# A fused decoder block: four buffers for split weights, later modulation loads on POOL, and accumulator banks that end one by one

## The chip, the cores and the metric

The kernel runs on one core of a Trainium2 chip, as one launch. The metric is the device time of that launch in microseconds (us). The core has several engines that run their own instruction streams: TensorE (PE, matrix products), VectorE (DVE), ScalarE (ACT), GpSimd (POOL) and SyncE (SP). DMA transfers are issued by one of these streams (here SP and POOL) and run beside them. An instruction waits on semaphores until what it needs is there; behind a waiting instruction its whole engine stands.

## The reference

One decoder block over 2048 tokens of width 1024. A vector c sets six modulation vectors (48 columns of 128 values); the first two shift and scale the first normalised input, the others serve the later parts. One combined projection feeds two groups of heads, gated linear attention (GLA) and dilated attention. Their outputs are joined, projected, and a gated feed-forward part follows.

```python
cond = jax.nn.silu(c)
mod = (cond @ w_ada[l] + b_ada[l])[:, None, :]
sh1, sc1, g1, sh2, sc2, g2 = jnp.split(mod, N_MOD, axis=-1)

h = rms_norm(x, norm1_g[l]) * (1 + sc1) + sh1
proj = h @ w_in[l]
gq, gk, gv, gr, glr, aq, ak, av = jnp.split(proj, split_at, axis=-1)
log_a = jax.nn.log_sigmoid((glr @ gla_w_gate[l] + gla_b_gate[l])) / GLA_GATE_TAU
y_gla = gla_group(gq, gk, gv, log_a, gr, gla_norm_g[l])
y_att = dilated_attention_group(qa, ka, av)      # qa, ka: rms_norm of aq, ak
mixed = jnp.concatenate([y_gla, y_att], axis=-1)
x = x + g1 * (mixed @ w_out[l])

h = rms_norm(x, norm2_g[l]) * (1 + sc2) + sh2
u = causal_depthwise_conv(h @ w_up[l], conv_w[l], conv_b[l])
u_gate, u_val = jnp.split(u, 2, axis=-1)
x = x + g2 * ((silu(u_gate) * u_val) @ w_down[l])
```

Widths in the combined projection: gq and gk 256 each, gv and gr 512 each, glr 16, aq, ak and av 512 each; the feed-forward part is 2816 wide.

## The kernel before

*Tiling.* The 2048 tokens are worked in four chunks of 512 (numbered 0 to 3). Activations lie with their 1024 channels as eight tiles of 128 partitions by 512 tokens. A large product is made of three matmuls for each tile (`mm3`, L288 to L290): activation and weight are each split into a high half of reduced precision and the low rest, and high by high, high by low and low by high are summed in one accumulator. The names `hhi`, `hlo` are the halves of an activation, `whi`, `wlo` those of a weight.

*Split weights.* Every weight block comes through `wslot`: a load of 512 KB into one of two raw buffers (`wraw`, L220, issued by POOL), a cast to the high half on ACT (L226), a subtraction for the low half on DVE (L227). The halves stand in three buffers each. `plan` lists all blocks in the order of use; `weights` gives out the next block, and before that starts the preparation of blocks up to `ahead=2` further on in the list. A raw buffer is free again when cast and subtraction have read it; a split buffer is free when the block's last matmuls have read it.

*The projections of one chunk.* `proj` runs the combined projection in an order written out by hand (`ORDER0` for chunk 0, `ORDER` for the others). `q0` to `q7` are queries and keys of the dilated heads (`qk`), `g0` to `g3` queries and keys of GLA (`glaqk`), `V0` and `V1` the values with the gate input (`av`), `W0` is gv and `W1` is gr (`wide`). `ORDER` begins with `W0` and both lists end with `W1`; so W1 of one chunk and W0 of the next one meet. I call this place the hand-over. There are four PSUM banks named `psg` for the accumulators of all large products, taken in turn, and four named `psa` for the small ones. A query or key block takes one `psg` bank; its drain is a square and a copy on ACT.

*wide.* It takes all four `psg` banks, one for each 128 tokens. For each of four weight blocks j, two tiles i, and four banks s, it issues one `mm3`; so each block is 24 matmuls of 128x512. The banks are drained at the end: for W0 by a copy on ACT (L497); for W1 by a tanh on ACT (L493), an addition and multiplication on DVE that reads the bank a last time (L494), and a multiplication by the norm's gain (L495). The result goes to memory by a DMA on SP (L498).

*The next chunk's input.* Between W1's last matmul and its drains, `hook` calls `begin(c + 1)`, which writes the normalisation and modulation of the next chunk: for each of eight tiles a product on DVE (L413), the high half on ACT (L415) and the low half on DVE (L417).

*Later modulation.* Modulation columns 16 to 47 aren't needed by the first projections. `ada_late` computes them beside the projections: 32 columns in two halves each, 64 loads of 128x512 (`wada`, L348, issued by SP) into buffers of the pool that the query blocks and Newton's steps use too (tags `ghi` and `glo`, five buffers each). Each half is multiplied by `cond` and summed on DVE (L355) two steps after its load; after a column's second half its bias is added (L332).

*What sets the order.* The code of the streams is interleaved by generators: `along` and `beside` advance one generator a set number of steps for each step of another. While the projections of chunks 1 to 3 are written, the attention of chunk 0 (`mix`, lines 579 to 800 in what follows) is interleaved with them. A scheduler then fixes the order of instructions on every engine when the program is built (`schedule_with_timeline_sim=True`): it works with modelled durations. So a change of buffers or dependencies moves many instructions on all engines.

After the projections follow, chunk by chunk, the output projection and the feed-forward part, with the attention of the next chunk beside them.

## Time and profile before

| what | value |
|---|---|
| median of three runs | 2660.18 us (2659.1 to 2661.48) |
| the profiled execution, its own time | 2663.11 us |
| its span in the trace | 2661.4 us |
| mean granted clock of TensorE | 0.992 |
| large matmuls in the three forms of `mm3` at 128x512 | 2040 each |
| weight blocks split on ACT and DVE (L226, L227) | 391 |
| moved by software queues (POOL's loads) | 203.71 MB |
| moved by hardware queues (SP's) | 198.40 MB |

The span is what the profiler recorded from the first to the last instruction; the execution's own time is 1.7 us longer. A busy share is an average over a start-up, a stage of projections (about 60 to 740 us), and a long stage of output and feed-forward products. The granted clock is the share of its full rate that TensorE was allowed to run at; the mean hides short stretches at half of it. In the views, `out<-in` are the names of buffers, "x" counts instructions, and "<-" with an engine and a line names what ended a wait.

### The profile page before, as it was taken

Reading aid. Unit: us, or ns where it says so; the run is one execution under the profiler, and the core shown is the slowest. Engines: PE = TensorE matmul, PEld = TensorE weight load, DVE = VectorE, ACT = ScalarE, POOL = GpSimd, SP = SyncE. Lnnn points to the kernel's source line nnn. Section 1 sums busy time; section 2 is a strip of 40 time slices with the busy share of each in tenths; the row PEclk is TensorE's granted clock in tenths of the full one; section 3 lists DMA queues with packets and bytes.
Section 4 is the critical chain, followed back from the end, with each engine's and each line's share of the span. In section 5 each row is a group of like instructions: output and inputs, shape, how many; then the busy total and the mean of one; then the engine's idle time right before and its main releaser. Section 6 shows DMA issues by size and latency. Waiting matters only on the chain.

```text
span 2661.4 us, 46859 instructions
## 1 busy us (share of the span) xinstructions
PE 2583.6 (97%) x18152; PEld 2116.1 (80%) x18152; DVE 1920.8 (72%) x4120; ACT 1274.0 (48%) x2607; POOL 209.1 (8%) x396
## 2 busy tenths in 40 slices
PE   5989999999989999999999999999999999999999
PEld 3877878878868888887787888878888888788887
DVE  7585885766677777776896777779777766666666
ACT  4455556556545454553545444445455443433332
POOL 0000000000000000001000000000000000010000
PEclk9999999999989999999999999999999999999999
DMA  7765575755633234346434444553344445422222
GB/s 281 247 203 200 185 235 168 226 183 191 219 108 103 97 124 132 125 132 227 137 104 125 140 133 129 192 167 118 101 139 145 141 125 186 135 96 102 95 95 95
DMA packets 196736, 405.10 MB, mean 152 GB/s; under 512 B 19985, under 2 KB 70946, under 8 KB 195234
## 3 DMA queue, kind: packets, MB, share of 16 engines
q0 software_dynamic: 55872, 203.71, 23.2%
q1 hardware_dynamic: 140642, 198.40, 22.7%
q8 instruction: 143, 2.34, 0.4%
q14 instruction: 79, 0.65, 0.1%
HBM read 339.12 MB, written 62.91 MB: 151 GB/s over the span
## 4 chain that ended last, share of the span: by engine, by line
PE 82%; issue 5%; DMA 5%; DVE 5%; ACT 2%; POOL 0%; SPq 0%; DVEq 0%; POOLq 0%; ACTq 0%
PE psg L288 24%; PE psg L289 23%; PE psg L290 23%; PE psa L752 2%; PE psa L732 2%; PE psa L854 2%; DMA wada<-in_w_ada_dram 1%; PE psa L590 1%; DVE wlo L227 1%; DMA sq<-in_xT_dram 1%; PE psa L849 1%; DMA x<-x 1%; PE psa L768 1%; DVE x L966 0%; DMA wraw<-in_w_ch_dram 0%
## 5 line engine op out<-in xcount | busy, mean ns | idle before, releaser
L288 PE MATMUL psg<-hhi,whi 128*128 128x512 f32 x2040 | 809.5, 399 | 15.9 <-ACT hhi L415 9.9
L289 PE MATMUL psg<-hlo,whi 128*128 128x512 f32 x2040 | 805.7, 395 | 2.7 <-DVE hlo L417 2.6
L290 PE MATMUL psg<-hhi,wlo 128*128 128x512 f32 x2040 | 804.0, 394 | 0.7 <-DVE wlo L227 0.7
L226 ACT CAST whi<-wraw 128x1024 fp32r<-128x1024 f32 (+1 forms) x391 | 409.9, 1049 | 472.2 <-PE psg L289 396.0
L227 DVE TENSOR_TENSOR wlo<-wraw,whi 128x1024 fp32r<-128x1024 f32 (+1 forms) x391 | 478.6, 1224 | 206.2 <-ACT whi L226 200.6
L288 PEld LDWEIGHTS psg<-hhi,whi 128*128 128x128 f32 x2040 | 385.6, 189 | 105.8 <-ACT hhi L415 13.3
L289 PEld LDWEIGHTS psg<-hlo,whi 128*128 128x128 f32 x2040 | 386.6, 190 | 85.9 <-DVE hlo L417 5.9
L290 PEld LDWEIGHTS psg<-hhi,wlo 128*128 128x128 f32 x2040 | 386.5, 189 | 83.0 <-DVE wlo L227 1.9
L288 PE MATMUL psg<-ghi,whi 128*128 128x512 f32 x704 | 279.5, 398 | 0.0
L289 PE MATMUL psg<-glo,whi 128*128 128x512 f32 x704 | 277.3, 394 | 0.0
L290 PE MATMUL psg<-ghi,wlo 128*128 128x512 f32 x704 | 276.0, 392 | 0.0
L966 DVE SCALAR_TENSOR_TENSOR x<-psg,mod,x 128x512 f32<-128x512 f32 x192 | 142.9, 748 | 117.3 <-PE psg L290 115.4
L288 PE MATMUL psg<-whi,hhi 128*128 128x512 f32 (+2 forms) x512 | 172.8, 347 | 12.3 <-DVE stg L494 7.9
L289 PE MATMUL psg<-wlo,hhi 128*128 128x512 f32 (+2 forms) x512 | 176.2, 345 | 5.7 <-DVE wlo L227 5.7
L220 POOL DMA_DIRECT2D wraw<-in_w_up_dram x176 | 92.9, 528 | 1080.6 <-DVE wlo L227 969.2
L290 PE MATMUL psg<-whi,hlo 128*128 128x512 f32 (+2 forms) x512 | 175.3, 343 | 0.0
L288 PEld LDWEIGHTS psg<-ghi,whi 128*128 128x128 f32 x704 | 132.3, 188 | 32.0 <-issue 4.6
L290 PEld LDWEIGHTS psg<-ghi,wlo 128*128 128x128 f32 x704 | 132.3, 188 | 28.2 <-issue 1.2
L289 PEld LDWEIGHTS psg<-glo,whi 128*128 128x128 f32 x704 | 132.4, 188 | 27.9 <-issue 2.1
L742 ACT ACTIVATE big<-big,nm 128x256 f32<-128x256 f32 (+1 forms) x256 | 122.4, 480 | 58.7 <-DVE nm L757 58.7
L921 ACT ACTIVATE y<-psg,conv_b_sb,conv_w_sb 128x512 f32<-128x512 f32 x176 | 135.8, 773 | 4.8 <-PE psg L290 2.3
L923 DVE SCALAR_TENSOR_TENSOR y<-psg,conv_w_sb,y 128x510 f32<-128x510 f32 x176 | 130.9, 744 | 0.7
(206 smaller groups left out, 3369.5 us busy)
## 6 DMA issues: line engine op xcount, KB each, us to landing
wraw<-in_w_up_dram POOLq DMA_DIRECT2D x176, 512.0 KB, 3.6
wraw<-in_w_down_dram POOLq DMA_DIRECT2D x88, 512.0 KB, 3.5
wraw<-in_w_ch_dram POOLq DMA_DIRECT2D x44, 512.0 KB, 4.5
wada<-in_w_ada_dram SPq DMA_DIRECT2D x74, 256.0 KB, 4.8
v<-v SPq DMA_DIRECT2D x68, 256.0 KB, 5.3
wraw<-in_w_tokw_dram POOLq DMA_DIRECT2D x32, 512.0 KB, 4.4
wraw<-in_w_out_dram POOLq DMA_DIRECT2D x32, 512.0 KB, 4.7
sq<-in_xT_dram SPq DMA_DIRECT2D x48, 256.0 KB, 4.4
```

The lines of the kernel that those rows point to most:

```text
L220: (nc.gpsimd if self.planned else nc.sync).dma_start(raw[:, :n], src)
L226: nc.scalar.copy(hi[:, :n], raw[:, :n])
L227: nc.vector.tensor_tensor(lo[:, :n], raw[:, :n], hi[:, :n].bitcast(F32), op=ALU.subtract)
L288: nc.tensor.matmul(ps, wh, hh, start=first and k == 0, stop=False, skip_group_check=shared)
L289: nc.tensor.matmul(ps, wh, hl, start=False, stop=False, skip_group_check=shared)
L290: nc.tensor.matmul(ps, wl, hh, start=False, stop=k == n - 1, skip_group_check=shared)
L732: nc.tensor.matmul(at(i, hh, z), q[H[hh], i * P:(i + 1) * P], key(H[hh], i, z), start=True, stop=True, skip_group_check=True)
L742: nc.scalar.activation(t[:, lo:hi], t[:, lo:hi], AF.Exp, bias=nm[:, hh, g, i:i + 1], scale=2.0 ** -(h + 1), accum_out=dn[:, hh, g, i:i + 1])
L752: nc.tensor.transpose(ps[:n, i * P:(i + 1) * P], part(S[hh], i), self.C("id"))
L921: nc.scalar.activation(y, ps, AF.Identity, bias=self.cb[:, b:b + 1], scale=self.cw[:, 2, b:b + 1])
L923: nc.vector.scalar_tensor_tensor(y[:, 2:], ps[:, :T - 2], self.cw[:, 0, b:b + 1], y[:, 2:], op0=ALU.mult, op1=ALU.add)
L966: nc.vector.scalar_tensor_tensor(x1, ps, self.mod[:, 40 + cb:41 + cb], x1, op0=ALU.mult, op1=ALU.add)
```

## The change

The diff does five things.

- The split weights have four buffers for each half, and `weights` prepares three blocks ahead (two for the second block of `av`, one before).
- The 64 late modulation loads are issued by POOL, on the queue that loads the weights.
- Each late modulation reduction waits for the matmul that `mm3` issued last when the code of the reduction was written (`self.lastmm`). So a reduction can't be placed ahead of the block beside which it was written.
- In `wide` the last block's eight `mm3` are sorted by bank: both tiles of bank 0, then those of bank 1, 2 and 3. The normalisation of the next chunk (`hook`) is written behind the drains.
- A scratch area for DMA descriptors is set to 4096 bytes, which frees room for the buffers.

```diff
@@ -135,8 +135,8 @@
         pool = lambda name, bufs, **kw: ctx.enter_context(tc.tile_pool(name=name, bufs=bufs, **kw))
         self.const = pool("const", 1)
         self.wraw = pool("wraw", 2)
-        self.whi = pool("whi", 3)
-        self.wlo = pool("wlo", 3)
+        self.whi = pool("whi", 4)
+        self.wlo = pool("wlo", 4)
         self.hp = pool("hp", 9)
         self.gp = pool("gp", 5)
         self.xp = pool("xp", 8)
@@ -268,7 +268,7 @@
                 yield from down(5)
             yield from ffn(c)
 
-    def weights(self, name, *idx, ahead=2):
+    def weights(self, name, *idx, ahead=3):
 
         while len(self.wready) <= self.wpos + ahead and self.wleft:
             n, i, k, m = self.wleft.pop(0)
@@ -287,7 +287,7 @@
             (wh, wl), (hh, hl) = ws[k], hs[k]
             nc.tensor.matmul(ps, wh, hh, start=first and k == 0, stop=False, skip_group_check=shared)
             nc.tensor.matmul(ps, wh, hl, start=False, stop=False, skip_group_check=shared)
-            nc.tensor.matmul(ps, wl, hh, start=False, stop=k == n - 1, skip_group_check=shared)
+            self.lastmm = nc.tensor.matmul(ps, wl, hh, start=False, stop=k == n - 1, skip_group_check=shared)
 
 
     def ada_setup(self):
@@ -345,14 +345,16 @@
             if n < len(parts):
                 b, j = parts[n]
                 raw = self.gp.tile([P, T], F32, name="wada", tag=("ghi", "glo")[j])
-                ld = nc.sync.dma_start(raw, self.A["w_ada"][b][:, cols(j)])
+                ld = nc.gpsimd.dma_start(raw, self.A["w_ada"][b][:, cols(j)])
                 if not n:
                     self.after(ld)
                 raws.append(raw)
             if n >= 2:
                 b, j = parts[n - 2]
                 raw, m = raws[n - 2], self.mod[:, b:b + 1]
-                nc.vector.tensor_tensor_reduce(raw, raw, self.cond[:, cols(j)], 0.5, m if j else 0.0, ALU.mult, ALU.add, m)
+                t = nc.vector.tensor_tensor_reduce(raw, raw, self.cond[:, cols(j)], 0.5, m if j else 0.0, ALU.mult, ALU.add, m)
+
+                self.tc.add_manual_dep(t.ins, self.lastmm.ins.name, mybir.DependencyInfo(mybir.DependencyClass.Sync, mybir.DependencyReason.DATA))
                 if j:
                     self.ada_end(b)
             yield
@@ -478,15 +480,16 @@
             pss = [self.pg() for _ in range(4)]
             for j in range(4):
                 w = self.weights("w_tokw", b, j)
-                for i in range(2):
-                    for s in range(4):
-                        h, l = hs[2 * j + i]
-                        tk = slice(s * P, (s + 1) * P)
-                        self.mm3(pss[s], [(h[:, tk], l[:, tk])], w[i:i + 1], i == 0 and j == 0, True)
+                order = [(i, s) for i in range(2) for s in range(4)]
+                if j == 3:
+
+                    order.sort(key=lambda x: x[1])
+                for i, s in order:
+                    h, l = hs[2 * j + i]
+                    tk = slice(s * P, (s + 1) * P)
+                    self.mm3(pss[s], [(h[:, tk], l[:, tk])], w[i:i + 1], i == 0 and j == 0, True)
                 if j < 3:
                     yield
-            if b == 1 and hook:
-                hook()
             for s in range(4):
                 st = stage()
                 if b:
@@ -496,11 +499,13 @@
                 else:
                     nc.scalar.copy(st, pss[s])
                 nc.sync.dma_start(D["rg" if b else "gv"][s * P:(s + 1) * P, :], st)
+            if b == 1 and hook:
+                hook()
             yield
 
         def av(b):
             n = 256 if b else 272
-            w = self.weights(f"w_av{b}", 0) + self.weights(f"w_av{b}", 1, ahead=1)
+            w = self.weights(f"w_av{b}", 0) + self.weights(f"w_av{b}", 1, ahead=2)
             if b:
                 pss = [self.pg() for _ in range(2)]
                 for i in range(KD):
@@ -1098,7 +1103,7 @@
     from concourse.bass_utils import run_bass_kernel_spmd as _run
 
     arrs = layout(**{n: np.asarray(a) for n, a in inputs.items()})
-    nc = _bacc.Bacc("TRN2", target_bir_lowering=False, num_devices=1)
+    nc = _bacc.Bacc("TRN2", target_bir_lowering=False, num_devices=1, dynamic_dma_scratch_size=4096)
     A = {n: nc.dram_tensor(f"in_{n}_dram", a.shape, mybir.dt.from_np(a.dtype), kind="ExternalInput").ap() for n, a in arrs.items()}
     A["outT"] = nc.dram_tensor("out_0_dram", (NCH, KD, P, T), F32, kind="ExternalOutput").ap()
     with tile.TileContext(nc, **TC) as tc:
```

From L288 on lines are shifted: L413, L415 and L417 of before are L415, L417 and L419 now, L494 is L497 and the copy L497 is L500.

The order of instructions, first on VectorE at the hand-over from chunk 0 to chunk 1, just ahead of the first drain of gr. `wada` is a modulation load's buffer, `mod` the modulation, `sq` and `stg` are staging tiles, `kt` and `sbd` belong to the attention of chunk 0. Before:

```order
L355 ISA wada,mod<-wada,cond 128x512
L355 ISA mod 128x1
L355 ISA wada,mod<-wada,cond,mod 128x512
L355 ISA mod 128x1
L641 COPY sbd_485<-kt 32x2x2x32
L641 COPY sbd_487<-kt 32x2x2x32
L355 ISA wada,mod<-wada,cond,mod 128x512
L355 ISA mod 128x1
L413 SCALAR_TENSOR_TENSOR sq<-sq,G_110,rstd 128x512
L227 TENSOR_TENSOR wlo<-wraw,whi 128x1024
L494 SCALAR_TENSOR_TENSOR stg<-stg,psg 128x512
```

In the changed program, at the same place:

```order
L227 TENSOR_TENSOR wlo<-wraw,whi 128x1024
L332 TENSOR_TENSOR mod<-mod,b_ada_sb 128x1
L355 ISA wada,mod<-wada,cond 128x512
L355 ISA mod 128x1
L579 COPY kt<-psa 128x512
L415 SCALAR_TENSOR_TENSOR sq<-sq,G_110,rstd 128x512
L606 TENSOR_TENSOR kt<-psa,consts_sb 128x128
L455 SCALAR_TENSOR_TENSOR stg<-stg,kgs,sq 128x512
L606 TENSOR_TENSOR kt<-psa,consts_sb 128x128
L497 SCALAR_TENSOR_TENSOR stg<-stg,psg 128x512 x4
```

The low half of a weight stands earlier, one modulation reduction instead of three stands in the rows ahead of the first drain, some of the attention's work has moved there, and the four drains (now L497) stand one behind the other.

Second, POOL's queue from W1 of chunk 0 on. Here `in_w_tokw` are the blocks of W0 and W1, `in_w_av` those of V0 and V1, `in_w_ch` those of queries and keys. Before:

```order
L220 DMA wraw<-in_w_av_dram 128x1024 x2
L220 DMA wraw<-in_w_ch_dram 128x1024 x4
L220 DMA wraw<-in_w_tokw_dram 128x1024 x8
L541 MEMSET glr 32x512
L220 DMA wraw<-in_w_av_dram 128x1088 x2
```

In the changed program (one block of W1 and a modulation load stand ahead of these rows; with it they hold the eight blocks of W1 and W0):

```order
L220 DMA wraw<-in_w_tokw_dram 128x1024 x4
L348 DMA wada<-in_w_ada_dram 128x512
L220 DMA wraw<-in_w_tokw_dram 128x1024
L348 DMA wada<-in_w_ada_dram 128x512 x8
L220 DMA wraw<-in_w_tokw_dram 128x1024
L348 DMA wada<-in_w_ada_dram 128x512
L220 DMA wraw<-in_w_tokw_dram 128x1024
```

Weight loads and modulation loads are mixed now, with up to eight modulation loads ahead of one weight block.

Third, VectorE near the end of W1 of chunk 2, in a stretch beside the attention of chunk 0 (`xm` and `nm` belong to it). Before:

```order
L417 SCALAR_TENSOR_TENSOR hlo<-sq,mod,hhi 128x512
L355 ISA wada,mod<-wada,cond 128x512
L355 ISA mod 128x1
L355 ISA wada,mod<-wada,cond,mod 128x512
L355 ISA mod 128x1
L227 TENSOR_TENSOR wlo<-wraw,whi 128x1024
L332 TENSOR_TENSOR mod<-mod,b_ada_sb 128x1
L417 SCALAR_TENSOR_TENSOR hlo<-sq,mod,hhi 128x512
L227 TENSOR_TENSOR wlo<-wraw,whi 128x1024
```

In the changed program:

```order
L355 ISA wada,mod<-wada,cond 128x512
L355 ISA mod 128x1
L415 SCALAR_TENSOR_TENSOR sq<-sq,G_110,rstd 128x512 x2
L227 TENSOR_TENSOR wlo<-wraw,whi 128x1024
L415 SCALAR_TENSOR_TENSOR sq<-sq,G_110,rstd 128x512
L799 TENSOR_TENSOR xm<-md,consts_sb 128x64
L419 SCALAR_TENSOR_TENSOR hlo<-sq,mod,hhi 128x512 x2
L227 TENSOR_TENSOR wlo<-wraw,whi 128x1024
L497 SCALAR_TENSOR_TENSOR stg<-stg,psg 128x512
```

One reduction instead of two stands ahead of the low halves here, and between the two low halves stand parts of the next chunk's normalisation.

## The prediction

> **What bounds the kernel now.** I read the page's first lines, the waits of TensorE (PE), the windows of the projection stage, and the timelines of PE and VectorE (DVE) there.
>
> ```profile
> span 2661.4 us, 46859 instructions
> PE 2583.6 (97%) x18152; PEld 2116.1 (80%) x18152; DVE 1920.8 (72%) x4120; ACT 1274.0 (48%) x2607; POOL 209.1 (8%) x396
> ```
>
> PE sets the end: it is busy for 97% of the span, so 2661.4 - 2583.6 = 77.8 us is all that it idles. Only that, and stretches at a lower clock, can be won.
>
> ```profile
> PE psa L400 <- DVE rstd L394: 17.5, 2, 14.6
> PE psg L288 <- ACT hhi L415: 9.9, 5, 4.3
> PE psg L288 <- DVE stg L494: 7.9, 3, 5.7
> PE psg L289 <- DVE wlo L227: 5.7, 3, 3.1
> PE psg L288 <- ACT stg L497: 1.9, 2, 1.4
> ```
>
> Each row gives the total, the number and the longest wait. The first two are the start and the change-over to the output projection, which the change does not touch. The other three are its targets: the drain of gr's banks (L494), the low half of a split weight (L227), the drain of gv's banks (L497): 7.9 + 5.7 + 1.9 = 15.5 us.
>
> ```profile
> 60.00:180.00 120.00, 117.45 (x664) 99.53 (x664) 74.70 (x119) 65.66 (x102) 10.04 (x19) 1.00 0.70 230
> 180.00:200.00 20.00, 12.63 (x130) 9.60 (x129) 19.96 (x43) 10.56 (x20) 2.12 (x4) 0.74 0.51 179
> 534.00:550.00 16.00, 11.43 (x46) 8.89 (x47) 12.84 (x25) 12.05 (x28) 1.58 (x3) 0.89 0.46 147
> 2300.00:2600.00 300.00, 299.46 (x1320) 247.38 (x1319) 195.38 (x307) 110.55 (x136) 28.52 (x55) 1.00 0.29 98
> ```
>
> Columns: stretch, length, busy time of PE, weight loads, DVE, ScalarE (ACT) and POOL, PE's granted clock, DMA share, GB/s. From 2300 to 2600 PE idles 0.5 us, so deeper buffering has nothing to win in the last stage. In 180 to 200 DVE is busy 19.96 of 20 us while PE works 12.63: there DVE is the bound. That is the hand-over from W1 of chunk 0 (the gr projection) to W0 of chunk 1 (gv); 534 to 550 is that from chunk 2 to 3.
>
> ```profile
> 182.73 0.76 PE L289 MATMUL psg<-wlo,hhi 128*128 128x512 f32 x1 [1.67 <-DVE wlo L227]
> 195.57 0.79 PE L288 MATMUL psg<-whi,hhi 128*128 128x512 f32 x1 [5.70 <-DVE stg L494]
> 221.02 0.39 PE L288 MATMUL psg<-whi,hhi 128*128 128x272 f32 x1 [1.39 <-ACT stg L497]
> 364.91 0.50 PE L288 MATMUL psg<-whi,hhi 128*128 128x512 f32 x1 [0.49 <-DVE stg L494]
> 535.66 0.50 PE L289 MATMUL psg<-wlo,hhi 128*128 128x512 f32 x1 [3.11 <-DVE wlo L227]
> 544.71 0.80 PE L288 MATMUL psg<-whi,hhi 128*128 128x512 f32 x1 [1.68 <-DVE stg L494]
> ```
>
> In brackets stands PE's wait and what ended it. They come in pairs, a late weight and then a late drain, at 182/195, at 365 and at 535/545. The third weight wait, by the total above, is 5.7 - 1.67 - 3.11 = 0.9 us.
>
> ```profile
> 182.80:186.20 3.40, 3.40 (x8) 2.71 (x9) 3.40 (x9) 0.00 (x0) 0.53 (x1) 0.50 0.70 222
> 193.10:199.80 6.70, 4.23 (x10) 3.36 (x11) 6.70 (x14) 3.39 (x5) 1.06 (x2) 0.50 0.52 196
> 544.70:548.00 3.30, 3.29 (x8) 2.62 (x9) 3.30 (x7) 3.30 (x7) 0.53 (x1) 0.50 0.04 13
> ```
>
> The granted clock is 0.50 in these stretches, which follow the waits of 1.67, 5.70 and 1.68 us. Each of about 3.4 us costs 1.7 us more, the double one up to 3.4.
>
> The Trainium skill ("TensorE: Matmul & The Clock Gate", What's actually happening) lets the clock fall only after a whole idle window of some 3.4 us. By that, the waits of 1.67 and 1.68 us would cost themselves alone, and the 3.4 us of clock in the sum below would be 0 (9.0 us instead of 12.4). The trace shows 0.50 behind both, so the measurement decides.
>
> **The change part by part.** Durations by the distance from one start to the next:
>
> ```profile
> 186.68 0.69 DVE L613 TENSOR_TENSOR pt<-kt,pt 128x512 f32<-128x512 f32 x1
> 187.28 0.69 DVE L614 TENSOR_TENSOR pt<-kt,pt 128x512 f32<-128x512 f32 x1
> 182.60 0.28 DVE L601 TENSOR_TENSOR kt<-psa,consts_sb 128x128 f32<-128x128 f32 x1
> 182.80 0.68 DVE L355 CUSTOM_DVE_ANT_0 wada<-wada,cond 128x512 f32<-128x512 f32 x1
> 533.09 0.69 DVE L355 CUSTOM_DVE_ANT_0 wada<-wada,cond 128x512 f32<-128x512 f32 x1
> 533.70 0.75 DVE L355 CUSTOM_DVE_ANT_0 wada<-wada,cond,mod 128x512 f32<-128x512 f32 x1
> 534.38 1.23 DVE L227 TENSOR_TENSOR wlo<-wraw,whi 128x1024 fp32r<-128x1024 f32 x1
> 535.51 0.16 DVE L332 TENSOR_TENSOR mod<-mod,b_ada_sb 128x1 f32<-128x1 f32 x1
> 535.58 0.75 DVE L417 SCALAR_TENSOR_TENSOR hlo<-sq,mod,hhi 128x512 fp32r<-128x512 f32 x1
> 536.24 1.23 DVE L227 TENSOR_TENSOR wlo<-wraw,whi 128x1024 fp32r<-128x1024 f32 x1
> 194.85 0.67 DVE L494 SCALAR_TENSOR_TENSOR stg<-stg,psg 128x512 f32<-128x512 f32 x1
> 195.45 0.73 DVE L417 SCALAR_TENSOR_TENSOR hlo<-sq,mod,hhi 128x512 fp32r<-128x512 f32 x1
> 362.89 0.39 PE L288 MATMUL psg<-whi,hhi 128*128 128x512 f32 x1
> 363.12 0.39 PE L289 MATMUL psg<-wlo,hhi 128*128 128x512 f32 x1
> 189.11 0.76 PE L590 MATMUL psa<-pt 64*32 64x32 f32 x64
> ```
>
> So a DVE operation on 128x512 takes 0.60 (two full tensors, or a drain L494) or 0.66 (one with a scalar column, L413/L417/L453), a modulation reduction 0.61 or 0.68, a low half 1.13, L601 0.20, a bias 0.07. PE takes 0.23 per 128x512 matmul and 0.76 for 64 small ones.
>
> *Hand-over of chunk 0.* In the changed program the last W1 bank still runs all its 24 matmuls at the end of W1, since it waits for a query bank's copy. The first tied modulation reduction waits for this bank's sixth matmul, 18 before the end. Everything behind it on DVE stands in order: from it to the first drain (L497 now) are three reductions (0.61 + 0.68 + 0.61), two low halves (2.26), five operations of 0.66 (3.30), two of Newton's (1.20), one bias (0.07), a copy from PSUM (0.60), two L606 (0.40) and the drain (0.60): 10.3 us. PE has 18 x 0.23 = 4.1 and 0.6 us of small matmuls meanwhile, so the first matmul of W0 still waits about 10.3 - 4.7 = 5.6, with hand-offs **5.9 us**. Before, it was 1.67 + 5.70 = 7.4: 1.5 us are won. The four drains stand together now and the modulation reductions between them are gone, but the tie itself makes DVE start this run late. The weight wait of 1.67 goes, as the last W1 block's low half now stands ahead of the reductions: 1.7 us of clock are won, the double stretch stays.
>
> *Drain of gv.* The last block's matmuls go bank by bank, so the first bank is done 3 x 6 matmuls = 4.1 us ahead of the last, and its copy on ACT is hidden by them. Both waits go: **1.9 us**.
>
> *Hand-over of chunk 1.* From the end of a run of small matmuls to the first drain stand 17 DVE operations: three low halves (3.39), seven of 0.66 (4.62), three of 0.60, one reduction (0.61), three of 0.20 (0.60): with the drain among the 0.60 about 11.0 us, against 41 matmuls of W1 (9.3) and 1.1 us of small ones: about 0.6 us left of 0.9 + 0.49: **0.8 us**.
>
> *Hand-over of chunk 2.* The low half that PE waited for (534.38) stood behind two reductions; it now stands a block earlier, and from the reduction tied to W1's last block to the drain are 7.0 us of DVE work (0.61, five of 0.66, two of 1.13, 0.22, 0.60) against 42 matmuls and small ones, 10.4 us. Both waits go, 3.11 + 1.68 = **4.8 us**, and 1.7 us of clock.
>
> Sum: 1.5 + 1.7 + 1.9 + 0.8 + 4.8 + 1.7 = 12.4 us won.
>
> *What it adds.* No arithmetic. The 64 late modulation loads move from SP to POOL:
>
> ```profile
> L348 SPq DMA_DIRECT2D wada<-in_w_ada_dram x60: 327/432/1681, 93.7 to 665.2; - x60
> DMA to landing us min/median/max: 2.9/4.5/8.1
> L220 POOL DMA_DIRECT2D wraw<-in_w_tokw_dram x32 | 16.9, 528 | 232.0 <-DVE wlo L227 174.3 <-DVE kt L601 20.0 <-DVE mod L332 19.0
> wraw<-in_w_tokw_dram POOLq DMA_DIRECT2D x32, 512.0 KB, 4.4
> ACT whi L226 <- PE psg L289: 396.0, 183, 9.8
> ```
>
> POOL issues one in 0.53 us: 64 x 0.53 = 34 us on an engine that is busy 8%, hidden by its long waits for a free raw buffer; SP is relieved of 64 x 0.43 = 28 us. Queued behind them are weight loads. The tightest is the third block of W0 behind eight modulation loads: its raw buffer is free 4.3 us after the tied matmul (0.61 + 0.60 + 0.66 + 0.68 + 1.13 and hand-offs), it lands 4.4 later and is cast 1.05 later, at 9.8 us; its first use is 12 matmuls into W0, at 4.7 + 5.9 + 2.7 = 13.3. Cover: 3.5 us; cost taken 0. Without that cover it is the slower rival. The ties add 64 semaphore waits on DVE; no row prices them, the bounds are 0 (DVE has slack outside the hand-overs) and the whole 5.9 us that one costs above; beyond what is counted I take 1.0. Eight reductions more fall in the last chunk's projections, 8 x 0.65 = 5.2 us of DVE beside PE: 0. The smaller descriptor scratch has no row: 0 if the loads run two deep as now, and at worst a load at a time, 92 weight loads x 4.9 + 64 x 5.0 = 770 us in a stage of 600. I take 0, as two raw buffers keep the weights at two loads. Moving the next chunk's normalisation behind the drains costs 0: W0's first operands stand ahead of them in the order.
>
> The Trainium skill ("SBUF — State Buffer", SBUF: two separate sides) speaks against POOL's queue: while VectorE copies fp32 in SBUF, POOL cannot write descriptors. Here POOL's issues average 528 ns with DVE 72% busy, so the trace does not bear it out; by the rule the rival below would come sooner, and the sum would be its 2667.
>
> Net 11.4 us: 2663.11 of the profiled execution (2661.4 and 1.7 around it) becomes 2651.7. The median shown, 2660.18, lies 2.9 lower: **2649 us**.
>
> **The rivals.**
> - *The splits do not come earlier.* ACT's cast waits for PE's release of a buffer 183 times (396 us), and with three ahead in four buffers it still waits for the block before. Against it: the low halves stand further ahead in the order. The weight terms fall out (1.67 counts within chunk 0's 1.5, so 1.5 + 1.7 + 0.3 + 3.1 = 6.6): 2655.6.
> - *DVE stays the bound.* If its operations cannot keep up behind the ties, the drains stay as late as now; only gv's drain and half of chunk 2's are won, about 4 us: 2656.
> - *All goes.* If DVE comes early to the tied run and chunk 0's hand-over closes too, 5.9 + 3.4 more: 2640.
> - *POOL's queue is late (slower).* The eight, seven and nine modulation loads at the three hand-overs wait for buffers whose reductions are tied to PE. If that holds the weight load behind them more than 3.5 us past its free buffer, it slips one block: 24 x 0.23 = 5.5 us and 1.7 of clock, three times, 21.6, less 11.4 won: 2649 + 21.6 - 3 (the queue's own wait is in part the drain's) = 2667.
>
> **How the numbers follow.** Forecast 0.48, all gone 0.10, splits not earlier 0.10, DVE the bound 0.15, POOL late 0.17. Within 0.2% (about what can be told from no change) is 2654.9 to 2665.5. Faster: 0.48 + 0.10 = 0.58; same: 0.25; slower: 0.17. The range runs from 2640 less 1 for the spread of the runs to the before's own 2661.5, so it leaves out the last rival and little else: 2639 to 2662.
>
> **What would show it.** Right: the waits for L227 and for gv's copy (now L500) in the PE waits near 0; one wait of about 6 us left at chunk 0's hand-over, ended by L497; clock 1.00 at the weight waits and at chunk 2's hand-over; POOL's weight loads still waiting mainly for L227. Wrong: PE waits that end with a cast L226 whose raw buffer came late, POOL waiting on modulation loads, or DVE idle at a tied reduction while PE waits.

## The result, and the profile after

The changed kernel took 2639.96 us, the median of four runs (2636.93 to 2641.08), against 2660.14 us before. The ratio is 0.9917 with a 95% interval of 0.9906 to 0.9929, some 22 us of 2660. The forecast was 2649 us, so the direction was right and the size about half. The median lies just inside the stated range (2639 to 2662); the ratio, applied to the median of before, gives 2638.1 us and lies just outside.

The first lines of the page of the changed kernel (span, and busy time of each engine):

```profile
span 2637.7 us, 46896 instructions
PE 2575.8 (98%) x18152; PEld 2114.0 (80%) x18152; DVE 1921.7 (73%) x4120; ACT 1276.3 (48%) x2607; POOL 243.8 (9%) x460
```

The span is 23.7 us shorter. TensorE does the same 18152 matmuls and idles 2637.7 - 2575.8 = 61.9 us where it idled 77.8: 15.9 us less. It is busy 7.8 us less with the same matmuls, in part by the clock (below). This split moves from one execution to the next: in a repeat of the changed kernel (`after_rep`, span 2635.3 us) TensorE is busy 2577.2 us and idles 58.1.

Where it was won is read from the matmuls done up to the first matmul of W0 behind a hand-over. The windows of TensorE from the start to that point (length, busy time and count of PE first), before for the hand-overs of chunk 1 and chunk 2 and the change-over to the output projection:

```profile
0.00:364.91 364.91, 320.77 (x2330) 261.20 (x2331) 265.76 (x508) 189.12 (x313) 26.22 (x53) 0.97 0.66 224
0.00:544.71 544.71, 492.31 (x3456) 402.03 (x3457) 393.43 (x834) 298.82 (x563) 39.40 (x78) 0.98 0.65 217
0.00:781.10 781.10, 720.42 (x5264) 590.12 (x5265) 552.91 (x1216) 425.79 (x828) 58.06 (x113) 0.98 0.63 208
```

and in the changed kernel:

```profile
0.00:352.69 352.69, 316.03 (x2331) 260.30 (x2331) 266.71 (x495) 194.90 (x322) 48.66 (x94) 0.99 0.69 234
0.00:526.42 526.42, 487.16 (x3456) 401.50 (x3457) 392.97 (x816) 304.05 (x568) 71.61 (x137) 0.99 0.68 226
0.00:759.24 759.24, 712.78 (x5265) 587.89 (x5265) 556.13 (x1217) 426.94 (x826) 93.40 (x178) 0.99 0.64 214
```

The counts agree to one matmul, so the times compare: 12.2 us are won by the first mark, 18.3 by the second, 21.9 by the third. All but 1.8 us of the 23.7 came from the stage of projections and what leads up to it, the stage that the forecast named.

The hand-overs in the timeline of TensorE of the changed kernel:

```profile
187.89 0.80 PE L288 MATMUL psg<-whi,hhi 128*128 128x512 f32 x1 [5.83 <-DVE stg L497]
352.69 0.51 PE L288 MATMUL psg<-whi,hhi 128*128 128x512 f32 x1 [0.37 <-DVE stg L497]
380.77 0.40 PE L288 MATMUL psg<-whi,hhi 128*128 128x272 f32 x1 [1.27 <-ACT stg L500]
526.42 0.50 PE L288 MATMUL psg<-whi,hhi 128*128 128x512 f32 x1 [0.55 <-DVE stg L497]
```

One large wait is left, at chunk 0's hand-over. Chunk 2's pair of 3.11 and 1.68 us is down to 0.55, chunk 1's of 0.88 and 0.49 to 0.37. Of gv's two waits, the one at chunk 1 is gone, the one at chunk 2 has grown from 0.50 to 1.27; in the repeat neither is there. No matmul at a hand-over waits for a low half.

The other waits of TensorE between 60 and 760 us, before (total, number, longest):

```profile
PE psa L590 <- DVE pt L614: 3.2, 2, 2.4
PE psg L288 <- ACT stg L470: 2.5, 2, 1.5
PE psa L445 <- DVE sqr L439: 1.8, 2, 1.6
PE psa L797 <- DVE xm L794: 1.2, 1, 1.2
PE psa L590 <- issue: 1.0, 1, 1.0
PE psg L288 <- ACT hhi L890: 0.9, 1, 0.9
PE psa L732 <- DVE md L738: 0.9, 1, 0.9
PE psa L768 <- DVE wlo L227: 0.8, 1, 0.8
PE psa L444 <- ACT sqr L438: 0.7, 1, 0.7
```

and in the changed kernel:

```profile
PE psa L402 <- DVE rstd L396: 3.8, 1, 3.8
PE psg L288 <- ACT hhi L895: 1.9, 1, 1.9
PE psa L737 <- DVE md L743: 0.8, 1, 0.8
PE psg L288 <- ACT stg L444: 0.8, 1, 0.8
PE psg L290 <- DVE wlo L227: 0.8, 1, 0.8
PE psg L288 <- ACT stg L472: 0.6, 1, 0.6
PE psa L446 <- ACT sqr L440: 0.4, 1, 0.4
PE psa L447 <- DVE sqr L441: 0.3, 1, 0.3
```

These are waits in the queries (sqr), in the attention (xm, md, and L768), at the copy that drains a GLA query or key block of the first projections (L470, now L472), at the copy that drains a query block (L444), and at the change-over: pt, the issue, L890 or L895, in the changed kernel also L402 (its counterpart of 2.9 us ends at 781.10 us before, outside that list) and the low half, which ends at 732.87 us. The forecast gave none of them a term. Without the change-over they were 2.5 + 1.8 + 1.2 + 0.9 + 0.8 + 0.7 = 7.9 us and are 0.8 + 0.8 + 0.6 + 0.4 + 0.3 = 2.9.

### The profile page after: what moved, and what is told of

It is laid out like the page before. It is cut to its first block, busy times and chain, and to the rows that moved or that the text cites. A ratio compares the mean times of both kernels' runs of the same rounds, so it can differ in the third digit from the quotient of the medians.

```text
span 2637.7 us, 46896 instructions
## 1 busy us (share of the span) xinstructions
PE 2575.8 (98%) x18152; PEld 2114.0 (80%) x18152; DVE 1921.7 (73%) x4120; ACT 1276.3 (48%) x2607; POOL 243.8 (9%) x460
## 3 DMA queue, kind: packets, MB, share of 16 engines
q8 instruction: 143, 2.34, 0.4%
## 4 chain that ended last, share of the span: by engine, by line
PE 88%; DVE 4%; DMA 4%; ACT 2%; issue 1%; SPq 0%; POOL 0%; DVEq 0%; ACTq 0%; POOLq 0%
PE psg L288 26%; PE psg L289 25%; PE psg L290 25%; PE psa L757 2%; PE psa L737 2%; PE psa L859 2%; DMA wada<-in_w_ada_dram 1%; PE psa L595 1%; DVE wlo L227 1%; DMA x<-x 1%; PE psa L773 1%; PE psa L854 1%; PE psa L666 1%; DMA sq<-in_xT_dram 1%; PE psa L665 1%
## 5 line engine op out<-in xcount | busy, mean ns | idle before, releaser
L288 PE MATMUL psg<-hhi,whi 128*128 128x512 f32 x2040 | 807.5, 398 | 16.5 <-ACT hhi L417 8.6
L288 PEld LDWEIGHTS psg<-hhi,whi 128*128 128x128 f32 x2040 | 386.0, 189 | 104.6 <-ACT hhi L417 10.7
L288 PE MATMUL psg<-ghi,whi 128*128 128x512 f32 x704 | 279.6, 398 | 0.0
L288 PE MATMUL psg<-whi,hhi 128*128 128x512 f32 (+2 forms) x512 | 175.3, 345 | 9.4 <-DVE stg L497 6.8
L288 PEld LDWEIGHTS psg<-ghi,whi 128*128 128x128 f32 x704 | 132.3, 188 | 31.8 <-issue 4.0
```

Of the source, the lines that this page charges most:

```text
L288: nc.tensor.matmul(ps, wh, hh, start=first and k == 0, stop=False, skip_group_check=shared)
```

## Experiments

Each kernel ran beside the kernel before on the same chip; ratios are to that. A ratio's interval is about +- 0.0012, that is 3 us, so differences below some 4 us between two kernels aren't told apart. "Gain" is 1 minus the ratio, times 2660 us.

### One part undone

*Buffers* (`u_buf`):

```diff
-        self.whi = pool("whi", 4)
-        self.wlo = pool("wlo", 4)
+        self.whi = pool("whi", 3)
+        self.wlo = pool("wlo", 3)
-    def weights(self, name, *idx, ahead=3):
+    def weights(self, name, *idx, ahead=2):
-            w = self.weights(f"w_av{b}", 0) + self.weights(f"w_av{b}", 1, ahead=2)
+            w = self.weights(f"w_av{b}", 0) + self.weights(f"w_av{b}", 1, ahead=1)
```

> The changed kernel with three split buffers and two blocks ahead again (one for the second block of av); all else as changed. Theory A, the buffers took away the waits for a low half: the waits of TensorE for L227 at the three hand-overs (1.67 + 0.88 + 3.11 = 5.7 us before) come back with one stretch of half clock (1.7 us), so some 7 us above the changed kernel, about 2647 us. Rival B, the tie did it, since it took the modulation reductions out from in front of the low halves: no wait over 0.8 us for L227 in the projections, and 2640 +- 2 us.

Measured 2654.29 us (ratio 0.9984, 0.9975 to 0.9992). The wait for a low half is back at chunk 0's hand-over, and the drain behind it is later too, in TensorE's timeline of this kernel:

```profile
184.79 0.50 PE L289 MATMUL psg<-wlo,hhi 128*128 128x512 f32 x1 [2.02 <-DVE wlo L227]
197.33 0.80 PE L288 MATMUL psg<-whi,hhi 128*128 128x512 f32 x1 [7.03 <-DVE stg L497]
```

So theory A is right that this wait comes back and wrong about the size: not 7 us but some 18 (0.9984 against 0.9917), of which the waits for low halves are a small part. At chunks 1 and 2 the weight waits stayed away, so B has a part in it.

*Ties* (`u_tie`):

```diff
-                self.tc.add_manual_dep(t.ins, self.lastmm.ins.name, ...)
```

> The changed kernel without the wait that ties each modulation reduction to a matmul; all else as changed. Theory A (buffers did it): the low halves stay on time, 2640 +- 2 us, and the wait at chunk 0's hand-over (5.8 us) shrinks or stays. Rival B (the tie did it): reductions stand in front of the low halves and drains again, the waits for L227 and for the drain of gr at chunk 2 come back, some 7 us, about 2647 us. Third, the tie itself makes VectorE late at chunk 0's hand-over: then the kernel without it is up to 5.8 us faster, about 2635 us.

Measured 2647.14 us (0.9955, 0.9942 to 0.9968). The third expectation named the right place: the wait at chunk 0 fell to 3.6 us. But the time rose by some 10 us all the same, and not by what B said, for no matmul waits for a low half by more than 0.2 us. Its waits of TensorE between 60 and 760 us begin:

```profile
PE psg L288 <- DVE stg L496: 4.2, 2, 3.6
PE psa L801 <- DVE xm L798: 3.6, 1, 3.6
PE psa L446 <- DVE sqr L440: 2.7, 2, 1.6
```

The waits of the attention (xm) and of the queries (sqr), 6.3 us, stand where the changed kernel has 0.7. What the ties do is seen in the windows of VectorE for the modulation reductions alone (L355), in the stretches ahead of the hand-overs of chunks 1 and 2. Before (length, busy time, instructions):

```profile
343.00:356.00 13.00, 6.42 (x18) 1.00 0.62 208
525.00:536.00 11.00, 5.85 (x18) 1.00 0.51 171
```

without ties in the changed kernel:

```profile
338.00:349.00 11.00, 5.65 (x16) 1.00 0.74 247
516.00:527.00 11.00, 5.58 (x18) 1.00 0.56 195
```

and in the changed kernel:

```profile
340.00:352.00 12.00, 1.46 (x4) 1.00 0.65 213
514.00:526.00 12.00, 0.69 (x2) 1.00 0.69 199
```

A reduction is two instructions here. Free ones come eight or nine at a time, on half of VectorE's time just ahead of a hand-over; tied ones come one or two. The other three kernels without ties (before, and `no_two` and `a_b4` below) have such bunches of seven to nine at the same two places; in the changed kernel no stretch of 10 us holds more than three.

*POOL's loads* (`u_sp`):

```diff
-                ld = nc.gpsimd.dma_start(raw, self.A["w_ada"][b][:, cols(j)])
+                ld = nc.sync.dma_start(raw, self.A["w_ada"][b][:, cols(j)])
```

> The changed kernel with the 64 modulation loads issued by SP again; all else as changed. Theory A: POOL's queue gives nothing and costs nothing, 2640 +- 2 us. Rival C, SP's relief of 64 issues is a part of the gain that the forecast left out (the stores and loads of the attention leave earlier): 2643 us or more, with waits for DMA or for tiles of the attention come back. Rival D, the loads on POOL cost weight blocks some time: 2637 us or less.

Measured 2640.92 us (0.9934, 0.9920 to 0.9948). D falls; A and C aren't told apart.

*Order of the banks and place of the normalisation* (`u_bank`):

```diff
-                if j == 3:
-                    order.sort(key=lambda x: x[1])
+            if b == 1 and hook:
+                hook()
             for s in range(4):
                 st = stage()
...
-            if b == 1 and hook:
-                hook()
             yield
```

> The changed kernel with the last block in the old order of banks and the next chunk's normalisation written ahead of the drains; all else as changed. Theory A: the waits for gv's copy come back (1.9 us before) and the drain of gr is late again at chunk 2 (1.68 us and 1.7 us of clock): some 5 us, about 2645 us. Rival B, what counts at the hand-overs is the work on VectorE alone: 2640 +- 2 us.

Measured 2638.78 us (0.9927, 0.9914 to 0.9940): B. gv's wait at chunk 2 is 0.60 us in this profile, less than the 1.27 with the new order, and the one at chunk 1 is gone here too. So it was not the order of the banks that took these waits away.

### The two large parts alone and together

`only_two` is the kernel before with buffers (with the smaller scratch) and ties, by the lines of the diff; `no_two` the changed kernel without them.

> The kernel before with two parts of the change alone: four split buffers with three blocks ahead (and the smaller descriptor scratch that makes room), and the ties. The modulation loads stay on SP, the banks in their old order, the normalisation ahead of the drains. Theory A, these two make the whole gain and the other two parts nothing: 2640 +- 2 us. Rival B, the other two help each other or replace one another, as each was undone with the other in place: 2644 us or more.

Measured 2645.51 us (0.9939, 0.9927 to 0.9952): B.

> The changed kernel without those two parts: three split buffers, two blocks ahead, no ties; loads on POOL, new order of banks and late normalisation stay. Theory A, buffers and ties add (14 and 7 us when undone one by one): the time of before, 2660 +- 3 us. Rival C, buffers and ties overlap, so that either one alone brings most: 2666 us or more would be needed for that, since 2654 and 2647 with one of them then are each more than half of the way; Rival D, they need each other: 2656 us or less.

Measured 2657.36 us (0.9984, 0.9974 to 0.9995). By the median alone that is in A's range; by the ratio, 2655.7 us of 2660, it is D's. The table below decides between them.

In `a_b4` and `a_tie` the kernel before has one of the two: two pools of four instead of three with the scratch, or the `lastmm` line and the tie.

> The kernel before with a fourth buffer for each split half (and the smaller descriptor scratch that makes room), and nothing else: two blocks ahead, no ties, loads on SP, old banks. If a free buffer is the larger part by itself (four buffers without the third block ahead gave 2639 with all else), some 13 us are won: 2647 us. Rival: without the ties the modulation reductions stand in front of the low halves as before, and the buffer alone gives only the weight waits of the forecast: 5.7 us and up to 3.4 of clock, 2651 to 2655 us.

Measured 2654.71 us (0.9986, 0.9977 to 0.9995). The weight waits are gone from the hand-overs, as both said; the time is the rival's.

> The kernel before with the ties and nothing else (three buffers, two ahead, loads on SP, old banks). If ties and buffers add, 7 us are won: about 2654 us, with the reductions no longer in front of the low half at chunk 2's hand-over (its wait of 3.11 us gone) and the wait at chunk 0's hand-over no shorter than before. Rival: the ties only pay where a fourth buffer lets the low halves use the room: 2660 +- 2 us.

Measured 2655.17 us (0.9987, 0.9977 to 0.9997). The wait of 3.11 us at chunk 2 is gone as expected. At chunk 0's hand-over the two waits are 2.34 and 3.09 us, together shorter than the 7.37 of before, which was not expected. The gain is between the two expectations.

With these, gains in us by the ratios:

| | neither | ties | buffers | both |
|---|---|---|---|---|
| loads on SP, old banks | 0 | 3.5 | 3.7 | 16.2 |
| loads on POOL, new banks | 4.3 | 4.3 | 12.0 | 22.1 |

Buffers and ties each give some 4 us alone, and 16 together: they don't add, each needs the other. Theory A of `only_two` fell too: POOL and banks bring 4 to 8 us more except beside ties alone, though neither cost more than 5 us when undone by itself. The interval of a step between the two lines is 3 to 4.5 us, so all but that beside ties alone stand clear of it; how they divide between POOL's loads, banks and the late normalisation stays open. The smaller scratch was not tried by itself: it stays in all kernels of the second line and comes with the buffers in the first.

### Free buffer or earlier place

`b4_a2` has the changed kernel's buffers and `ahead=2` (1 for the second `av` block), `b3_a3` its `ahead=3` and three buffers.

> The changed kernel with its four split buffers, but two blocks ahead in the code (one for the second block of av). Theory E, a buffer must be free and the split must also be written earlier: 2650 us or more. Rival F, the free buffer is what counts, since the cast on ACT waits for TensorE's release of it: 2640 to 2644 us.

Measured 2638.78 us (0.9917, 0.9905 to 0.9929): F, the same ratio as the changed kernel.

> The changed kernel with three split buffers, but three blocks ahead in the code. Both theories of the buffers say that the split can't come earlier without a free buffer: 2652 us or more, like three buffers and two ahead. Rival G, the place in the code alone brings it (the low half stands ahead of other VectorE work in the order): 2640 to 2646 us. Since the cast then waits for a buffer in front of other work on ACT, it may also be slower than before, over 2660 us.

Measured 2660.62 us (0.9998, 0.9985 to 1.0010). The earlier place without the room gains nothing over three buffers and two ahead (0.9984), and is perhaps slower; the intervals just overlap. So "three blocks ahead" in the change does nothing that can be measured; the fourth buffer does it.

### Where the ties work

Of the 64 reductions 19 are written beside W0 or W1. `tie_w` ties these, `tie_q` the 45 others:

```diff
             pss = [self.pg() for _ in range(4)]
+            self.inw = True
...
             yield
+            self.inw = False
...
+                if self.inw:
-                self.tc.add_manual_dep(t.ins, self.lastmm.ins.name, ...)
+                    self.tc.add_manual_dep(t.ins, self.lastmm.ins.name, ...)
```

(`if not self.inw` in `tie_q`.) The changed kernel ran once more beside them.

> The changed kernel as it is, beside the next three on the same chip. 2638 to 2641 us, ratio to before 0.991 to 0.993.

Measured 2637.06 us (0.9917, 0.9905 to 0.9929).

> The changed kernel with only the 19 ties of reductions that are written beside the wide blocks W0 and W1; the other 45 reductions are free. If the ties bring their 7 us at the hand-overs, as the forecast priced them, they are kept: 2638 to 2642 us. Rival: they bring them between the hand-overs, where free reductions crowd the queries' and the attention's work on VectorE: the waits for L440/L441 and for xm come back, about 2647 us, like the kernel without any tie.

Measured 2651.59 us (0.9971, 0.9960 to 0.9983), above even the 0.9955 of no tie at all, though the intervals overlap.

> The changed kernel with only the 45 ties outside the wide blocks; the 19 reductions beside W0 and W1 are free. If the ties bring their gain at the hand-overs, 2645 us or more. Rival, between the hand-overs: 2640 us or less, since at chunk 0's hand-over the free reductions can go earlier and its wait of 5.8 us falls towards the 3.6 us seen without ties.

Measured 2639.86 us (0.9926, 0.9914 to 0.9939); the wait at chunk 0 is 3.4 us. So the ties bring their gain by the 45 reductions written between the hand-overs. The rival's account of `tie_w` needs a correction, though. Its waits between 60 and 760 us begin (lines one to three later than in the changed kernel):

```profile
PE psg L289 <- DVE stg L500: 10.6, 3, 6.6
PE psg L289 <- ACT stg L503: 3.5, 1, 3.5
```

The reductions left free were written beside the queries, but TensorE waits in this kernel at the hand-overs, for the drains, and hardly in the queries (0.2 us).

### The wait that is left

`n_late` begins the later modulation behind chunk 0's projections, `n_v1` moves V1 of chunk 0 to just ahead of W1, `n_both` does both:

```diff
-        gemm = along(self.ada_late(), 66, chain(ahead(1), ahead(2), ahead(3), proj(3)), 98)
+        gemm = chain(ahead(1), along(self.ada_late(), 66, chain(ahead(2), ahead(3), proj(3)), 72))
-ORDER0 = "g0 g1 g2 g3 V0 q0 q1 W0 q2 q3 V1 q4 q5 q6 q7 W1".split()
+ORDER0 = "g0 g1 g2 g3 V0 q0 q1 W0 q2 q3 q4 q5 q6 q7 V1 W1".split()
```

> The changed kernel with the later modulation begun only after chunk 0's projections, its 64 halves spread over the other three chunks. Theory of the forecast: the wait of 5.8 us at chunk 0's hand-over is the work that stands on VectorE from the first tied reduction to the first drain; without it there the run starts earlier and is three reductions (1.9 us) shorter, the wait falls to 0 to 3 us, and the time to some 2635 us. Rival: what stands there is the normalisation, the low halves and Newton's steps, which wait for TensorE themselves: the wait stays at 5 us or more; and 15 halves more in chunks 1 to 3 (10 us of VectorE) may cost there: 2640 to 2646 us.

Measured 2637.59 us (0.9927, 0.9914 to 0.9939). The wait fell from 5.83 to 2.21 us:

```profile
185.53 0.80 PE L288 MATMUL psg<-whi,hhi 128*128 128x512 f32 x1 [2.21 <-DVE stg L497]
```

As expected the run of VectorE ahead of the drain is shorter, but it doesn't start earlier: in both kernels it starts 6.0 us before TensorE runs out of work. In time this kernel can't be told from the changed one (0.9917).

> The changed kernel with chunk 0's second value block V1 moved between the last key block q7 and W1, so that q7's Newton steps on VectorE are done before W1 ends. Theory of the forecast: two Newton steps and the scaling that follows (1.9 us) leave the run of VectorE ahead of the first drain, and the last bank no longer waits for a query block's copy; the wait of 5.8 us falls by 2 us or more: 2636 to 2638 us. Rival: the run is as long, since other work of the attention moves up: 2640 +- 2 us.

Measured 2632.87 us (0.9906, 0.9893 to 0.9918), four runs from 2632.08 to 2635.45. Here W0 of chunk 1 follows its W1 without a wait that the list shows at that place; its largest wait between 60 and 700 us is 1.2 us, and what remains for gr's drains is one line:

```profile
PE psg L288 <- DVE stg L497: 0.4, 1, 0.4
```

The theory holds for the wait. The time is below its range by the median and at its lower end by the ratio (2635 us of 2660).

> The changed kernel with both edits: V1 of chunk 0 between q7 and W1, and the later modulation begun after chunk 0. Theory: both shorten the same queue on VectorE ahead of the first drain of gr, and with V1 moved that wait is already gone (0.95 us left), so the second edit adds little there: within 2 us of the kernel with V1 moved alone, some 2632 us. Rival: the modulation's work in chunk 0 also costs elsewhere (the wait in chunk 1's queries), so both add: 2629 us or less.

Measured 2632.97 us (0.9904, 0.9890 to 0.9919), against 2637.06 for the changed kernel on the same chip. The theory holds: the second edit adds nothing that can be measured to the first. The two versions with V1 moved have the lowest times of all, some 4 to 5 us below the changed kernel by the medians. Their intervals overlap with its own, so that is likely, not settled.

## Why the prediction was half right

**Chunk 0's hand-over: right in size, wrong in what starts the run.** The forecast counted 10.3 us on VectorE from the first tied reduction to the first drain's end, and a wait of 5.9. VectorE's timeline in the changed kernel, with the ends of that run and what stands ahead of it:

```profile
176.06 0.75 DVE L375 SCALAR_TENSOR_TENSOR nwt<-psa,eps,sq 128x512 f32<-128x512 f32 x1 [4.27 <-ACT sq L452]
...
177.40 0.69 DVE L355 CUSTOM_DVE_ANT_0 wada<-wada,cond 128x512 f32<-128x512 f32 x1
...
187.15 2.48 DVE L497 SCALAR_TENSOR_TENSOR stg<-stg,psg 128x512 f32<-128x512 f32 x4
```

With 0.60 for the first of four drains that is 187.75 - 177.40 = 10.35 us, without a gap, and the wait is 5.83. Of 7.37 us 1.5 were won, as forecast. But it is not "the tie itself" that "makes DVE start this run late". The reduction shows no wait of its own: VectorE had waited 4.27 us for ScalarE (L452), for the last key block's Newton step, and began at 176.06. In `u_tie`, without ties, it begins behind the same wait (4.26 us), 5.8 us before TensorE runs out of work, against 6.0 here. That both ways come to about the same start is luck. The experiments agree: without ties or without modulation in chunk 0 the run is shorter and the wait 3.6 and 2.2 us; with V1 moved, so that this Newton step comes earlier, it is gone.

**Chunks 1 and 2: right.** 1.0 us won where 0.8 were forecast, 3.11 + 1.68 - 0.55 = 4.2 where 4.8.

**Drain of gv: not by its cause.** 1.9 us were forecast; 1.39 + 0.50 - 1.27 = 0.6 came in this profile and all of it in the repeat. But with the old order of banks 1.3 of it comes as well, and that order costs nothing that can be measured.

**Ties and VectorE between the hand-overs: the step that failed.** The forecast bounded the ties' cost below by 0, as "DVE has slack outside the hand-overs", took 1.0 us for it, and gave the waits of the queries and the attention no term. But slack over a stage doesn't say how the work is spread in it. Undone, the ties cost some 10 us, so they are a gain and not a cost; 45 of them, written outside the wide blocks, carry nearly all of it.

Two things set the kernels without these 45 ties apart. One is the bunches. The other is that a free reduction stands in VectorE's order before its load has landed, and the engine waits for it. VectorE's waits at the reductions between 60 and 760 us, for before, for `tie_w`, and (two rows) for the changed kernel:

```profile
DVE wada L355 <- DMA wada<-in_w_ada_dram: 19.0, 12, 3.6
DVE wada L356 <- DMA wada<-in_w_ada_dram: 16.3, 9, 3.7
DVE wada L355 <- PE psg L290: 25.5, 18, 4.1
DVE wada L355 <- DMA wada<-in_w_ada_dram: 3.8, 2, 2.0
```

The waits for such loads are 15.6 to 19.3 us in the four kernels without ties and in `tie_w`, and 1.4 to 5.3 in every kernel with the 45 ties. The ties make VectorE wait for TensorE instead, 25.5 us in the changed kernel. Chunk 2's hand-over of before shows both things at once:

```profile
524.59 0.69 DVE L355 CUSTOM_DVE_ANT_0 wada<-wada,cond 128x512 f32<-128x512 f32 x1 [3.30 <-DMA wada<-in_w_ada_dram]
```

From there VectorE works without a gap, with the bunch in it, to the low half at 534.38 us that TensorE waited for; the forecast saw two reductions in front of it, not this wait of 3.30. `tie_w` has no such bunch (at most five reductions in 10 us) and loses all the same, which speaks for the waits for loads. But no run shows what else VectorE could have done in these waits, or changes one thing without the other, so which of them makes the 10 us stays open.

In the list of TensorE's other waits, 3.0 of the 5.0 us (7.9 to 2.9) are those of xm and sqr. xm's wait is there in three of the four kernels without any tie (1.2 us before, 2.4 in `a_b4`, 3.6 in `u_tie`, none in `no_two`) and in no kernel with all ties. sqr's is 2.3 to 3.6 us without ties, but also up to 2.4 with ties and three buffers and 1.6 in `n_v1`; ahead of that of before (1.64 us) stands a low half and no reduction, so the ties are not shown to be its cause. The copy of the first projections (L470 or L472) goes with the buffers: 1.5 to 4.3 us in the five kernels with three, 0 to 1.1 with four, except 2.9 and 2.5 in `n_late` and `n_both`.

**Buffers: right in mechanism, and not to be summed alone.** The wait for low halves went. "The splits do not come earlier" falls by `u_buf`, and `b4_a2` shows that it is the room, not the lead in the code. But without the ties the room gives only 4 us, or 8 beside POOL's loads and the new banks.

**POOL: the cover held.** Two rows of POOL in the changed kernel (count, busy time, mean ns, idle time before, its releasers):

```profile
L348 POOL DMA_DIRECT2D wada<-in_w_ada_dram x64 | 34.7, 545 | 52.3 <-DVE mod L332 16.5 <-PE psa L446 16.3 <-DVE G L336 6.7
L220 POOL DMA_DIRECT2D wraw<-in_w_tokw_dram x32 | 17.0, 531 | 167.5 <-DVE wlo L227 127.2 <-DVE mod L332 12.5 <-DVE stg L455 7.0
```

The loads cost 34.7 us of POOL, as worked out, and the blocks of W0 and W1 still wait mainly for their raw buffer. The slower rival didn't come. Nor did "all goes": its time, 2640, is the measured one, but by luck, for its hand-over stayed.

**Clock: right at its places.** 3.4 us were forecast for the stretches that begin at 182.80 and 544.62 us, and neither has a successor; chunk 0's hand-over keeps its half clock, as forecast. From the start-up (62 us) to the third mark, TensorE's granted clock was 0.50 for 23.9 us before, 12.0 in the changed kernel and 17.8 in its repeat; that is up to 6.0 and 3.0 us less, as half of such a stretch is lost where TensorE is busy. Its busy time fell by 7.8 and 6.4 us. What makes up the rest isn't shown.

Together: 1.5 + 1.0 + 4.2 + 0.6 = 7.3 us of idle time at the forecast's places (9.0 in its sum), 5.0 in between (no term), 3.6 at the change-over, the start and the later stages (no term; what is left of 15.9), and 7.8 of busy time (3.4). The 1.0 of cost for the ties didn't come. That makes the 23.7 us of the spans where the forecast had 11.4.

## What to carry to other kernels

Work without a deadline (here the later modulation) is not free because its engine has slack on average. Look at where a scheduler puts it: whether it comes in bunches ahead of the places where that engine is waited for, and whether the engine stands in front of it until its data has landed. Tying each piece to a step of the critical engine spreads it and puts it later; here nearly all of the gain came from the pieces written between the hand-overs, and not from those at the hand-overs, where the forecast looked. Two edits to what one engine has to do (more room for the early work, less late work in front of it) were worth more than twice their sum here, so a sum of terms measured one by one was too low.

## What the runs showed of the hardware

The half-clock stretches lie on a grid. By the records of the granted clock those of before begin 182.80, 193.04, 264.72 and 544.62 us from the start: from one to the next 3, 21 and 82 times 3.413 us. The length of a single wait does not decide whether one follows. The windows of before, for the cells ahead of two such stretches and for one that no stretch followed:

```profile
179.40:182.80 3.40, 1.74 (x38) 1.17 (x37) 3.40 (x8) 2.40 (x7) 0.00 (x0) 1.00 0.56 190
531.00:534.40 3.40, 1.55 (x7) 0.94 (x5) 3.40 (x14) 1.33 (x2) 0.00 (x0) 1.00 0.32 87
541.20:544.60 3.40, 1.31 (x10) 0.96 (x10) 1.74 (x5) 3.37 (x6) 0.00 (x0) 1.00 0.22 60
```

A wait of 1.67 us was followed by half clock in the next cell, since other gaps stood beside it (TensorE was busy 1.74 of 3.40 us); the wait of 3.11 us that ended at 535.66 lay across two cells, and no half clock followed. Busy time in the cell doesn't decide it alone either: 1.55 us kept the clock, 1.74 did not. The ends of matmuls are modelled, so these windows don't show the bound. The Trainium skill ("TensorE: Matmul & The Clock Gate", What's actually happening) says that the window runs freely and lasts 3413 ns, and the trace agrees. That a whole window without matmuls is needed, as the forecast read it, doesn't agree with these cells.

The mean granted clock can mislead: the changed kernel's profile shows 0.994 and its repeat 0.991. The repeat has 13.65 us at half clock in the start-up (from 31.78 us) and the other none, yet TensorE is busy 31.0 and 30.9 us in the first 60 us: where it idles half the time, the half clock cost nothing that shows.

The Trainium skill ("SBUF — State Buffer", SBUF: two separate sides) advises against loads from POOL beside VectorE's copies. The changed kernel, with 64 loads more on POOL and VectorE busy 73% of the span, issues one in 545 ns, and undoing it gained nothing (0.9934 against 0.9917): no run here shows that cost. But VectorE's copies between SBUF tiles (L394, L459, L462, L644 and L646) take only 43.5 of its 1921.7 us in this kernel, so the runs hardly test the page, and the forecast's "the trace does not bear it out" says too much.
